# A hybrid two-layer trunk on one core: the order of its instructions from another simulator

## The chip, the cores and the metric

The kernel runs on one core of a Trainium2 chip, as one launch. The metric is the device time of one execution in microseconds (us); lower is better. Engines are named as in the profile: PE is TensorE's matmuls, PEld its weight loads, DVE is VectorE, ACT is ScalarE, POOL is GpSimd, and SP is SyncE, whose queue issues the DMAs.

## The reference

512 tokens of width 1024 pass two layers. Layer 0 mixes tokens with a Mamba-2 SSD block (inner width 2048, 32 heads in 4 groups, state 128, chunks of 128 tokens), layer 1 with HGRN2 (8 heads of 128). Each layer then has a layer norm, a squared-ReLU MLP of width 4096, a second layer norm, and a gate with per-layer input embeddings. All data is float32. Cut to what matters:

```python
for i in range(2):
    mix = ssd_mixer(x, ...) if i == 0 else hgrn2_mixer(x, ...)
    h = layer_norm(ALPHA * x + mix, ln_g[i, 0], ln_b[i, 0])
    h = layer_norm(ALPHA * h + square(relu(h @ w1[i])) @ w2[i], ln_g[i, 1], ln_b[i, 1])
    x = h + sigmoid(h @ ple_w_gate[i]) * (p[i] @ ple_w_proj[i])

# ssd_mixer: z, xbc, dt = split(x @ w_in); xbc = silu(causal_conv(xbc))
#   per chunk and head: y = (C B^T * decay) @ (x dt) + C @ carried_state + d * x
#   out = group_rms_norm(y * silu(z)) @ w_out
# hgrn2_mixer: q, f, v, g = split(x @ w_in); k = (1-lb) sigmoid(-f)
#   per head: causal scores of q and k under products of the forget gates, o = scores @ v
#   out = (rms_norm(o) * silu(g)) @ w_out
```

## The kernel before, in words

**Arithmetic.** Matmuls with weights are made to near float32 accuracy from three fast ones. A value is split into a rounded high part and a low rest, and `mm3` (L118 to L121) adds high x high, high x low and low x high in PSUM: the lines L119, L120 and L121. `unit` (L102) loads a 128 x 1024 weight tile with a DMA on SP's queue (`raw`, 3 buffers, L106) and `split` (L109) makes its high part on ScalarE (`whi`, L113) and its low part on VectorE (`wlo`, L115), with 6 buffers of each. A unit feeds 24 matmuls of 512 columns in `project` and 12 in a block product.

**Stages**, in program order:

- The SSD mixer. Input columns are projected tile by tile (`projected`, which calls `project`), convolved (`conv_silu`, L631 and L634) and passed to `core(j)`, 16 passes of two heads each. A pass transposes (`pt`, L693), weighs (`xw`, L700), makes chunk states (`pm`, L705), carries them (`pv`, L712 to L715), builds decays (L709, L721, L724), and makes two products (`yd` at L735, `yo` at L741) that end in `y` (L748 to L751) and a split (L800, L801). The pass of one pair of heads is traced behind the projections of the next. The block's output product adds into `acc` (L253).
- `norm` and `layer_norm` (L199 to L224), and `transpose_split` (L233, L237, L238), which brings the normalized rows back as split columns.
- The MLP: hidden tiles (L414, L416), then block products with sums of blocks on both sides (seven products in place of eight): `half_blocks` (L293 to L313) prepares the hidden side, `weight_sums` (L315 to L333) loads weights into `r` tiles and adds them on VectorE. `PERIODS` alternates hidden tiles and products. Then the gate (L487 to L499).
- `values4`, the first value products of the HGRN mixer, made in the same way.
- The HGRN mixer: `hcore` handles two heads at a time, four times. It climbs seven levels of growing blocks (L942 to L1046: short matmuls at L972, L980 and L987, VectorE products at L999 to L1012, copies by ScalarE at L1040 and L1046), makes states (L1054 to L1069), outputs (L1078 to L1090) and splits (L1098 to L1100). Between its steps, at 13 `yield`s per pair, `fill` issues background matmuls (projections of later heads, values, the output product) to an amount given in microseconds by `FILL`.
- The second layer norm, MLP and gate, and the output.

**What sets the order.** Nothing above fixes the engines' lists by itself. The kernel is traced as a program with tiles from pools; the tile scheduler then decides. It plays the program in a simulator. Whenever an engine there can take an instruction, it takes the one of best priority among those whose inputs are ready and whose output tile has a free buffer. The priority is the place in the traced program, moved forward by `tc.high_priority(offset=...)`: `LEAD` = 100 places for weight units, `SOON` = 40 for some evictions, `EARLY` = 60, `SUMS` up to 300 for the weight sums, `FIRST` = 1000 for the start. The order in which instructions left, engine by engine, becomes the program; semaphore waits are added after that, and on the chip each engine goes through its list as it stands.

Two parts are under a manual order for TensorE alone, `values4` and the whole HGRN mixer:

```python
with tc.manual_schedule(engines={mybir.EngineType.PE}):
```

There TensorE's list is the traced order; ScalarE, VectorE and SP remain with the scheduler.

## Time and profile before

| | us |
|---|---|
| median of 3 runs | 1425.95 |
| lowest and highest of the runs | 1424.66, 1426.19 |
| the profiled execution, its own time | 1424.0 |
| its span, first to last instruction | 1422.2 |
| PE busy | 1412.7 |
| PEld busy | 1172.5 |
| DVE busy | 1055.1 |
| ACT busy | 754.2 |

How to read it: the span is what the trace covers, and the execution's own time is 1.8 us longer. Busy times of different engines lie beside each other. PE's busy time has modelled ends, since matmuls are pipelined, so it alone doesn't tell whether TensorE works at its full pace. In the rows of the profile, a group is given by line, engine, operation and tiles; "idle before" is the time that the engine stood still just before the group's instructions, followed by what ended it. "Waits" have the total, the number of times and the longest.

### The profile page before, as it was taken

How to read it: one execution, taken by the hardware profiler on the slowest of the kernel's cores; microseconds unless marked ns; L12 is line 12 of the kernel's file. 1: busy time of each engine (PE TensorE's matmuls, PEld its weight loads, DVE VectorE, ACT ScalarE, POOL GpSimd, SP SyncE). 2: the span in 40 equal slices, each digit the busy share in tenths (PEclk: the TensorE clock that was granted, in tenths of full speed). 3: DMA queues.
4: the chain of work that ended last, by engine and by line, in shares of the span. 5: the costliest groups of instructions: out<-in, count | busy, mean ns of one | idle time of the engine just before them, and what ended most of it. 6: DMA issues, size and time to landing. Idle time of an engine off the chain costs nothing.

```text
span 1422.2 us, 20042 instructions
## 1 busy us (share of the span) xinstructions
PE 1412.7 (99%) x7869; PEld 1172.5 (82%) x7869; DVE 1055.1 (74%) x1736; ACT 754.2 (53%) x1134; POOL 1.9 (0%) x12
## 2 busy tenths in 40 slices
PE   9999999999999999999999999999999999999998
PEld 7888888888888888888888888877898888888887
DVE  8998687797966767677986576678695867667873
ACT  7776454563265454545545556655555444544641
POOL 0000000000000000000000000000000000000000
PEclk9999999999999999999999999999999999999999
DMA  8432323233333434344621421222163444434231
GB/s 313 138 124 90 120 87 121 102 115 127 145 119 120 161 133 149 133 146 166 214 83 49 133 90 60 75 90 90 46 236 104 148 140 142 149 133 163 89 119 45
DMA packets 49390, 178.00 MB, mean 125 GB/s; under 512 B 5520, under 2 KB 6288, under 8 KB 49168
## 3 DMA queue, kind: packets, MB, share of 16 engines
q1 hardware_dynamic: 49296, 176.73, 36.3%
q8 instruction: 62, 1.02, 0.3%
q14 instruction: 32, 0.26, 0.1%
HBM read 174.54 MB, written 2.16 MB: 124 GB/s over the span
## 4 chain that ended last, share of the span: by engine, by line
PE 94%; DVE 2%; ACT 2%; DMA 1%; issue 0%; ACTq 0%; DVEq 0%
PE pj L119 24%; PE pj L120 24%; PE pj L121 24%; PE py L119 5%; PE py L121 5%; PE py L120 5%; PE py L735 1%; PE pt L233 1%; PE py L741 1%; PE pm L705 1%; DMA raw<-in_wssd 1%; PE py L972 1%; PE pt L693 1%; PE py L1078 1%; DVE wlo L115 0%
## 5 line engine op out<-in xcount | busy, mean ns | idle before, releaser
L113 ACT CAST whi<-raw 128x1024 fp32r<-128x1024 f32 x222 | 232.9, 1051 | 323.5 <-PE pj L120 225.1
L119 PE MATMUL pj<-b,whi 128*128 128x512 f32 (+1 forms) x1006 | 382.3, 381 | 0.7 <-ACT b L237 0.7
L120 PE MATMUL pj<-b,whi 128*128 128x512 f32 (+1 forms) x1006 | 380.3, 378 | 0.0
L121 PE MATMUL pj<-b,wlo 128*128 128x512 f32 (+1 forms) x1006 | 379.3, 377 | 0.0
L115 DVE TENSOR_TENSOR wlo<-raw,whi 128x1024 fp32r<-128x1024 f32 x222 | 270.0, 1221 | 126.4 <-ACT whi L113 124.6
L119 PEld LDWEIGHTS pj<-b,whi 128*128 128x128 f32 x1006 | 188.8, 188 | 34.2 <-ACT b L237 0.9
L121 PEld LDWEIGHTS pj<-b,wlo 128*128 128x128 f32 x1006 | 189.1, 188 | 33.7
L120 PEld LDWEIGHTS pj<-b,whi 128*128 128x128 f32 x1006 | 189.2, 188 | 32.8 <-issue 0.9
L119 PE MATMUL pj<-whi,b 128*128 128x512 f32 x536 | 213.0, 398 | 0.0
L121 PE MATMUL pj<-whi,b 128*128 128x512 f32 x544 | 212.9, 392 | 0.0
L120 PE MATMUL pj<-wlo,b 128*128 128x512 f32 x536 | 210.2, 392 | 0.0
L121 PEld LDWEIGHTS pj<-whi,b 128*128 128x128 f32 x544 | 102.1, 188 | 21.0
L119 PEld LDWEIGHTS pj<-whi,b 128*128 128x128 f32 x536 | 100.7, 188 | 20.7 <-ACT b L1099 0.6
L120 PEld LDWEIGHTS pj<-wlo,b 128*128 128x128 f32 x536 | 100.8, 188 | 19.3
L113 ACT CAST whi<-r 128x1024 fp32r<-128x1024 f32 x72 | 75.8, 1053 | 67.7 <-PE pj L121 38.6
L115 DVE TENSOR_TENSOR wlo<-r,whi 128x1024 fp32r<-128x1024 f32 x72 | 87.7, 1220 | 20.6 <-ACT whi L113 19.9
L121 PE MATMUL py<-whi,b 128*128 128x512 f32 (+1 forms) x250 | 97.0, 388 | 0.0
L120 PE MATMUL py<-wlo,b 128*128 128x512 f32 x224 | 87.1, 389 | 0.0
L119 PE MATMUL py<-whi,b 128*128 128x512 f32 x224 | 87.1, 390 | 0.0
L121 PEld LDWEIGHTS py<-whi,b 128*128 128x128 f32 x250 | 46.9, 188 | 9.7
L634 DVE SCALAR_TENSOR_TENSOR cv<-pj,cst,cv 128x509 f32<-128x509 f32 (+2 forms) x66 | 48.7, 745 | 3.5 <-ACT cv L631 2.8
L119 PEld LDWEIGHTS py<-whi,b 128*128 128x128 f32 x224 | 42.0, 188 | 9.1 <-DVE sg L494 0.3
(292 smaller groups left out, 1850.8 us busy)
## 6 DMA issues: line engine op xcount, KB each, us to landing
raw<-in_w SPq DMA_DIRECT2D x112, 512.0 KB, 3.7
r<-in_w SPq DMA_DIRECT2D x64, 512.0 KB, 4.1
raw<-in_wssd SPq DMA_DIRECT2D x36, 512.0 KB, 3.8
a<-csd SPq DMA_DIRECT2D x16, 512.0 KB, 3.7
raw<-in_wso SPq DMA_DIRECT2D x16, 512.0 KB, 3.6
raw<-in_wg SPq DMA_DIRECT2D x16, 512.0 KB, 3.7
raw<-in_whq SPq DMA_DIRECT2D x16, 512.0 KB, 3.8
raw<-in_whvg SPq DMA_DIRECT2D x14, 512.0 KB, 3.7
```

Of the source, the lines that this page charges most:

```text
L113: nc.scalar.copy(hi[:, :n], f)
L115: nc.vector.tensor_sub(lo[:, :n], f, f32(hi[:, :n]))
L119: nc.tensor.matmul(out, sh, mh, start=start, stop=False, **kw)
L120: nc.tensor.matmul(out, sh, ml, start=False, stop=False, **kw)
L121: nc.tensor.matmul(out, sl, mh, start=False, stop=stop, **kw)
L233: nc.tensor.transpose(pt[:, j * P : (j + 1) * P], src[:, k * P : (k + 1) * P], ident)
L634: nc.vector.scalar_tensor_tensor(cv[:, d:], ps[:, : T - d], convw[:, i, k : k + 1], cv[:, d:], ALU.mult, ALU.add)
L693: nc.tensor.transpose(pt[:, c * P : (c + 1) * P], xs[:, c * P : (c + 1) * P], ident)
L705: nc.tensor.matmul(pst_[:, c * P : (c + 1) * P], btok[:, c, :], xw[:, c].rearrange("p h q -> p (h q)"), start=True, stop=True)
L735: nc.tensor.matmul(yd[64 * r : 64 * r + 64, sl], xdt[:, 2 * c + r, :], m[:, r, sl], start=True, stop=True)
L741: nc.tensor.matmul(yo[:, c * P : (c + 1) * P], pv[:, c - 1].rearrange("p h q -> p (h q)"), cm[:, c * P : (c + 1) * P], start=True, stop=True,)
L972: nc.tensor.matmul(pcs[r][bs, n * c : n * c + n], kk[r][:, ts], qs, start=True, stop=True)
```

## The change

One argument is given to the context in which the kernel is traced. The scheduler then plays the program in its other simulator, which keeps a timeline of events for each engine, its sequencer, its queues and the DMA engines, with semaphore waits and with times of its own for instructions and transfers. The rule of choice (best priority among what is ready), the program, the tiles, the buffers and the priorities are as before. The parts with a manual order for TensorE keep it.

```diff
@@ -1234,7 +1234,7 @@
     args["csd"] = nc.dram_tensor("csd", (32, T), F32).ap()
     args["out"] = nc.dram_tensor("out_0", (T, D), F32, kind="ExternalOutput").ap()
-    with _tile.TileContext(nc) as tc:
+    with _tile.TileContext(nc, schedule_with_timeline_sim=True) as tc:
         trunk(tc, args)
     r = _run(nc, [feeds], core_ids=[0])
```

## The prediction

> **What bounds the kernel now.** I read the page first: its span, the busy times, the slices of the granted clock and the chain of work that ended last.
>
> ```profile
> span 1422.2 us, 20042 instructions
> PE 1412.7 (99%) x7869; PEld 1172.5 (82%) x7869; DVE 1055.1 (74%) x1736; ACT 754.2 (53%) x1134; POOL 1.9 (0%) x12
> ...
> PEclk9999999999999999999999999999999999999999
> ...
> PE 94%; DVE 2%; ACT 2%; DMA 1%; issue 0%; ACTq 0%; DVEq 0%
> ```
>
> TensorE is the bound: busy for 99% of the span, 94% of the chain, with a granted clock of nine tenths or more in every slice. But its ends are modelled, so I asked the timeline whether "busy" hides slow issue. This is a quiet stretch late in the first mixer:
>
> ```profile
> 366.11 0.39 PE L119 MATMUL pj<-whi,b 128*128 128x512 f32 x1
> ...
> 366.34 0.39 PE L120 MATMUL pj<-wlo,b 128*128 128x512 f32 x1
> ...
> 366.57 0.39 PE L121 MATMUL pj<-whi,b 128*128 128x512 f32 x1
> 366.57 0.19 PEld L119 LDWEIGHTS pj<-whi,b 128*128 128x128 f32 x1
> ...
> 366.79 0.39 PE L119 MATMUL pj<-whi,b 128*128 128x512 f32 x1
> ```
>
> A 512-wide matmul starts every 0.227 us (0.68 us over three), and 0.19 us of each interval is its weight load. No order of the same matmuls changes that.
>
> [...]
>
> Next, the busy times by stretch, which I cut at the seams of the code: start, SSD mixer, first layer norm, MLP and gate with the value products, HGRN mixer, second seam, second MLP and gate, tail.
>
> ```profile
> core 0: us, PE busy (x) PEld busy (x) DVE busy (x) ACT busy (x) POOL busy (x), PEclk, DMA share, GB/s
> 0.00:16.00 16.00, 14.55 (x59) 11.47 (x59) 10.74 (x19) 10.09 (x18) 0.58 (x8) 1.00 0.88 339
> 16.00:370.00 354.00, 353.78 (x1986) 292.72 (x1986) 291.15 (x551) 205.49 (x272) 0.00 (x0) 1.00 0.37 128
> 370.00:390.00 20.00, 18.68 (x149) 17.79 (x148) 19.65 (x27) 6.21 (x11) 0.00 (x0) 1.00 0.33 106
> 390.00:830.00 440.00, 440.00 (x2007) 365.33 (x2007) 315.53 (x386) 231.58 (x304) 1.28 (x4) 1.00 0.40 133
> 830.00:1005.00 175.00, 172.66 (x1728) 140.21 (x1727) 125.83 (x375) 103.25 (x252) 0.00 (x0) 1.00 0.24 80
> 1005.00:1025.00 20.00, 19.71 (x98) 15.56 (x96) 13.48 (x35) 8.37 (x25) 0.00 (x0) 1.00 0.04 16
> 1025.00:1400.00 375.00, 375.00 (x1772) 314.24 (x1771) 274.31 (x341) 187.43 (x251) 0.00 (x0) 1.00 0.40 138
> 1400.00:1422.20 22.20, 18.30 (x87) 15.21 (x85) 4.38 (x8) 1.79 (x3) 0.00 (x0) 0.98 0.14 48
> sum 1422.20, PE 1412.68 PEld 1172.54 DVE 1055.07 ACT 754.23 POOL 1.86; mean PE 176.58 PEld 146.57 DVE 131.88 ACT 94.28 POOL 0.23
> ```
>
> TensorE is idle for 1422.20 - 1412.68 = 9.5 us in all: 1.45 at the start, 3.90 in the tail, and between them 0.22 + 1.32 + 2.34 + 0.29 = 4.17 us. The two MLP stretches, 815 us together, have none. So a new order has about 4 us to win and a whole kernel to lose.
>
> **The change part by part.** The program keeps its instructions, tiles and priorities. What moves is the order in which each engine's list is written, since that is the order in which the simulator let the instructions go. On the chip each engine runs its list as written; a wait at its head holds all that is queued behind it. So an edit costs something only where an instruction stands ahead of one that the chip could have run sooner, and only if TensorE then has nothing ready.
>
> *The weight feed, all stretches.* Each weight unit is a DMA on SP's queue (L106), a cast on ScalarE (L113) and a difference on VectorE (L115).
>
> ```profile
> L113 ACT CAST whi<-raw 128x1024 fp32r<-128x1024 f32 x222 | 232.9, 1051 | 323.5 <-PE pj L120 225.1
> L115 DVE TENSOR_TENSOR wlo<-raw,whi 128x1024 fp32r<-128x1024 f32 x222 | 270.0, 1221 | 126.4 <-ACT whi L113 124.6
> raw<-in_w SPq DMA_DIRECT2D x112, 512.0 KB, 3.7
> ```
>
> Refilling one unit takes 3.7 + 1.05 + 1.22 = 6.0 us from issue. How far ahead it runs is seen in what the casts waited for:
>
> ```profile
> L113 ACT CAST whi<-raw x222: 1029/1055/1068, 16.8 to 1389.7; 128x1024 fp32r<-128x1024 f32 x111
> L113 ACT CAST whi<-r x72: 1037/1055/1057, 436.0 to 1333.0; 128x1024 fp32r<-128x1024 f32 x72
> its engine sat idle before it (us, times) until:
>   PE pj L120: 232.4, 85
>   PE pj L121: 99.7, 59
>   PE py L121: 45.6, 49
> ```
>
> In 85 + 59 + 49 = 193 of 294 casts ScalarE stood waiting for TensorE to give a buffer back: the feed is held back by its six buffers. A unit feeds 24 matmuls (5.4 us at 0.227) in a projection and 12 (2.7 us) in a product, so five filled buffers are 14 to 27 us of work, against 6.0 us to refill. A cast or a load that is moved a few places, or an SP wait that holds the next loads a few us, stays hidden. I put the feed, and with it both MLP stretches, at 0. If that cover went, each missing unit would show up to 6.0 us.
>
> *SSD mixer (16 passes, TensorE's order also free).* TensorE visits each pass's short matmuls between projections that depend on nothing in the pass. A visit written too early waits for VectorE or ScalarE with the projections stuck behind it. Now such waits are small:
>
> ```profile
> PEld pm L705 <- DVE xw L700: 1.9, 11, 0.2
> PEld pt L693 <- ACT btok L662: 1.5, 4, 0.6
> ```
>
> Lower end: those 3.4 us and no more vanish. Upper end: each pass waits for one L115 that was put ahead of its operation, 16 x 1.22 = 19.5 us. I take one wait of L693's size per pass, 16 x (1.5 / 4) = 6.0 us, because visits placed with a margin are what the rows show; that is nearer to a small slip than to a whole L115.
>
> *HGRN mixer (4 pairs of heads, TensorE's order stays as traced).* Here only ScalarE, VectorE and SP move, while TensorE's list, with its fixed portions of background matmuls between the steps, does not. A pair has 13 such hand-overs, 52 in all. Lower end: the 2.34 us idle of that stretch are won. Upper end: an L115 ahead of the chain at every hand-over, 52 x 1.22 = 63 us. I take one per pair, 4 x 1.22 = 4.9 us; VectorE has 175.0 - 125.8 = 49 us unused there, so most displaced differences find a gap.
>
> *Table loads on ScalarE.* They sit between functions, and a new order can bring more or fewer.
>
> ```profile
> L709 ACT ACT_TABLE_LOAD x14 | 18.0, 1283 | 0.2
> ...
> 1004.07 0.22 ACT L1085 ACTIVATION_READ_ACCUMULATOR cbm<-py 128x1 f32 x1
> ...
> 1004.30 1.28 ACT L1086 ACT_TABLE_LOAD   x1
> ...
> 1005.60 0.30 ACT L1086 ACTIVATE hms<-hms,cst 128x4 f32<-128x4 f32 x1
> ```
>
> One costs 1.28 us on an engine that is 53% busy. It matters only as a late step of a chain, where it weighs like one L115, so it is inside the bounds above; I add 0.
>
> [...]
>
> *Seams, start and tail.* At the first layer norm VectorE is busy 19.65 of 20 us, and TensorE idles 1.32. The step there that could be displaced is this pair:
>
> ```profile
> L223 DVE SCALAR_TENSOR_TENSOR acc<-acc,lnmv,a 128x1024 f32<-128x1024 f32 x16 | 20.4, 1277 | 0.3 <-DVE lnmv L218 0.3
> L224 DVE SCALAR_TENSOR_TENSOR acc<-acc,lnrs,b 128x1024 f32<-128x1024 f32 x16 | 20.4, 1278 | 0.0
> ```
>
> Bounds -1.3 to +2.6 us; I take 0, and 0 for the start and the tail, where data in and out set the time.
>
> Sum: 6.0 + 4.9 = 10.9 us. The profiled execution took 1424.0 us (1422.2 of span and 1.8 around it), so 1434.9; the median of the runs, 1425.95, lies 1.95 above that execution, so I forecast 1436.9.
>
> **Rivals.** *Faster.* The other simulator's order suits the chip's timing better and TensorE's inner waits close. For it: greedy filling with projections is always possible in the SSD mixer. Against: only 4.17 us are there, 2.34 of them under a frozen TensorE list. It gives 1425.95 - 4.2 = 1421.8, by at most these 4 us.
>
> *No change.* Either the two orders nearly agree, or the buffers swallow every difference. For it: 193 blocked casts and no idle TensorE over 815 us. Against: two mixers whose short steps have no such buffers. It gives 1426.
>
> *The HGRN list breaks (slower, and outside my range).* The chain of a pair alternates between TensorE, VectorE and ScalarE, and the portions of background between steps are fixed. If the new order puts weight splits or evictions of the background ahead of chain steps as a rule, not once per pair, every hand-over waits. At 32 of 52 hand-overs it is 39 us, at all of them 63: 1425.95 + 6.0 + 63 = 1495. For it: the chain steps have the better priority only when they are ready in the simulator's own time. Against: VectorE's 49 spare us. It decides from about 8 displaced hand-overs on (8 x 1.22 = 10 us).
>
> [...]
>
> **How the numbers follow.** A modest loss as summed: 50%. The HGRN list breaks: 18%. No change: 15%. Faster: 17%. A measurement of this kernel tells about 0.2% (2.9 us) from no change; the runs spread from 1424.66 to 1426.19. The modest loss by itself runs from 1429 to 1475: above, SSD's 19.5, half the HGRN bound (27 of 63 would be 22 hand-overs) and a seam's 2.6 on 1425.95. Below, I let the range reach to 1420, the faster rival with the runs' spread. That leaves out most of the broken-list case above (about 13%) and a few per cent below.
>
> **What would show it.** In the changed kernel's profile: about 7869 matmuls again, the same 0.227 us pace, no idle TensorE in both MLP stretches (feed term 0). In the SSD stretch, waits of TensorE's weight loads on L700, L662 or L721 grown by about 6 us; in the HGRN stretch TensorE idle of about 7 instead of 2.34 us, ended by VectorE or ScalarE. I am wrong if the loss lies in the MLP stretches (the cover was not there), if a seam or the start is longer by over 3 us, if TensorE's clock falls, or if TensorE idles less than 7 us in all.

## The result, and the profile after

| us | before | after |
|---|---|---|
| median (lowest to highest of 4 runs each) | 1426.07 (1424.66 to 1427.10) | 1504.36 (1502.71 to 1507.23) |
| the profiled execution, its own time | 1424.0 | 1507.23 |
| its span | 1422.2 | 1505.5 |

The ratio is 1.0552, 95% interval 1.0531 to 1.0572. The forecast was 1436.9, its range 1420 to 1475: the sign was right, the size was not, and the time lies outside the range. The page of the changed kernel, the lines that answer to those shown first of before:

```profile
span 1505.5 us, 20089 instructions
PE 1440.5 (96%) x7869; PEld 1191.2 (79%) x7869; DVE 1055.7 (70%) x1736; ACT 777.6 (52%) x1151; POOL 1.9 (0%) x12
...
PEclk9999999999899999999989999999989999999999
...
PE 84%; DVE 9%; ACT 4%; issue 2%; DMA 1%; DVEq 0%; ACTq 0%
```

The same 7869 matmuls and 1736 VectorE instructions, but TensorE's share of the chain fell from 94% to 84%, VectorE's rose from 2% to 9%, and three of the 40 slices of the granted clock dropped to 8. TensorE is idle for 1505.5 - 1440.5 = 65.0 us (before 9.5), and its busy time grew by 1440.5 - 1412.7 = 27.8. The two, 55.5 + 27.8 = 83.3, are the whole growth of the span.

The busy times by stretch of the changed kernel say where. I cut it at its own seams, which come later and later than those of before (columns as in the table of before; the seventh entry of each row, after the five engines, is the granted clock):

```profile
16.00:60.00 44.00, 37.31 (x219) 30.25 (x219) 31.54 (x60) 34.84 (x42) 0.00 (x0) 0.92 0.53 196
60.00:370.00 310.00, 304.67 (x1652) 250.23 (x1651) 238.36 (x459) 186.40 (x236) 0.00 (x0) 0.99 0.30 101
370.00:393.50 23.50, 23.50 (x117) 19.22 (x116) 17.68 (x26) 8.12 (x11) 0.00 (x0) 1.00 0.62 224
393.50:420.00 26.50, 8.64 (x37) 6.75 (x37) 24.68 (x32) 4.16 (x8) 0.00 (x0) 0.61 0.25 79
420.00:433.00 13.00, 12.32 (x103) 11.89 (x102) 2.08 (x3) 1.89 (x4) 0.00 (x0) 1.00 0.01 1
433.00:750.00 317.00, 317.00 (x1442) 264.27 (x1441) 227.65 (x273) 158.46 (x201) 0.00 (x0) 1.00 0.44 143
750.00:770.00 20.00, 12.70 (x49) 9.54 (x49) 16.41 (x26) 8.20 (x17) 0.00 (x0) 0.74 0.54 157
770.00:820.00 50.00, 50.00 (x239) 41.30 (x238) 25.59 (x33) 21.11 (x30) 0.00 (x0) 1.00 0.17 54
820.00:840.00 20.00, 14.90 (x63) 11.62 (x62) 14.56 (x17) 11.69 (x18) 0.00 (x0) 0.83 0.16 56
840.00:1070.00 230.00, 227.69 (x1966) 186.02 (x1965) 153.76 (x411) 133.51 (x284) 1.28 (x4) 1.00 0.27 86
1070.00:1125.00 55.00, 42.48 (x231) 36.44 (x230) 38.74 (x69) 20.36 (x52) 0.00 (x0) 0.84 0.34 125
1125.00:1440.00 315.00, 315.00 (x1436) 262.87 (x1435) 221.91 (x269) 158.75 (x203) 0.00 (x0) 1.00 0.41 132
```

Length less PE busy is the idle time. The long matmul streams (433 to 750, 770 to 820, 1125 to 1440) have none, as before. Five short places have most of it: the start of the SSD 6.7, the first norm 17.9 + 0.7, the second norm 7.3, the transposes of the value products (L448) 5.1, the end of the HGRN mixer with the third norm 12.5. Each of them also has a granted clock below 1.0. The SSD between 60 and 370 has 5.3, and the body of the HGRN mixer 2.31, where before had 2.34.

TensorE's waits in the changed kernel (total, times, longest) name the same places:

```profile
PE pt L233 <- DVE b L238: 19.6, 6, 5.3
PE pt L233 <- issue: 8.7, 1, 8.7
PE pj L119 <- ACT b L237: 6.4, 5, 3.7
PE pj L119 <- ACT sz L683: 5.3, 3, 2.2
PE pt L448 <- DVE b L453: 4.9, 2, 3.0
PE py L666 <- ACT cm L635: 4.5, 1, 4.5
PE pt L233 <- DVE acc L224: 2.4, 1, 2.4
```

L233 is the transpose of the normalized rows in `transpose_split`, L237 and L238 its two evictions, L224 the last step of `layer_norm`: a few waits of several us, at seams, and not many small ones.

What happens there is read best from VectorE's timeline at the first norm (start, duration, instruction). First before, then after:

```profile
357.34 0.15 DVE L221 RECIPROCAL lnrs<-lnsd 128x1 f32<-128x1 f32 x1
357.41 0.73 DVE L253 SCALAR_TENSOR_TENSOR acc<-pj,ri,acc 128x512 f32<-128x512 f32 x1
358.06 1.28 DVE L224 SCALAR_TENSOR_TENSOR acc<-acc,lnrs,b 128x1024 f32<-128x1024 f32 x1
```

```profile
393.61 0.21 DVE L221 RECIPROCAL lnrs<-lnsd 128x1 f32<-128x1 f32 x2
393.74 1.20 DVE L327 TENSOR_TENSOR r<-r,r 128x1024 f32<-128x1024 f32 x1
394.87 0.68 DVE L207 BATCH_NORM_STATS2 lnst<-acc 128x6 f32<-128x512 f32 x1
395.47 1.20 DVE L115 TENSOR_TENSOR wlo<-raw,whi 128x1024 fp32r<-128x1024 f32 x1
396.59 0.74 DVE L253 SCALAR_TENSOR_TENSOR acc<-pj,ri,acc 128x512 f32<-128x512 f32 x1
397.26 1.21 DVE L330 TENSOR_TENSOR r<-r,r 128x1024 f32<-128x1024 f32 x1
398.39 2.35 DVE L115 TENSOR_TENSOR wlo<-raw,whi 128x1024 fp32r<-128x1024 f32 x2
400.66 0.74 DVE L253 SCALAR_TENSOR_TENSOR acc<-pj,ri,acc 128x512 f32<-128x512 f32 x1
401.32 2.46 DVE L224 SCALAR_TENSOR_TENSOR acc<-acc,lnrs,b 128x1024 f32<-128x1024 f32 x2
```

VectorE is never idle in either (busy 2.00 of 2.00 us from 357.34 to 359.34 before, 10.17 of 10.17 from 393.61 to 403.78 after). But between the reciprocal L221 and the L224 that needs it, before has one other instruction listed and after has eight (nine between the first L221 and its own L224): sums of weights (L327, L330), weight splits (L115), other rows' statistics (L207), output parts (L253). L224 starts 401.32 - 393.74 = 7.6 us later than it could. In TensorE's timeline over the same time the output product is used up and nothing else is left until the rows arrive (in brackets the idle time and what ended it):

```profile
393.56 0.39 PE L121 MATMUL pj<-whi,b 128*128 128x512 f32 x1
402.69 1.09 PE L233 MATMUL pt<-cst,acc 128*128 128x128 f32 x4 [8.74 <-issue]
409.11 1.12 PE L233 MATMUL pt<-cst,acc 128*128 128x128 f32 x4 [5.33 <-DVE b L238]
413.30 1.12 PE L233 MATMUL pt<-cst,acc 128*128 128x128 f32 x4 [3.08 <-DVE b L238]
```

In before the first of these transposes ran at 359.44 among output parts that were still left. "issue" in the first row stands for a wait with no releaser in the profile. By the times it was L224: the first of the two from 401.32 (1.23 us each) ends 0.1 us before 402.69.

Eight or nine instructions stand there only in the first two rows of the first norm. At the second and third norm L221 and L224 are about as close as before (0 to 4 instructions between them, before 1 to 3). At the second, the transposes start when TensorE's products have run out (the first L233 at 756.42, after 2.36 us of waiting; in before at 701.16, among products); what makes them late there was not taken apart.

### The profile page after: what moved, and what is told of

The parts are those of the page before. It is cut to its first block, busy times and chain, and to the rows that moved or that the text cites. A ratio compares the mean times of both kernels' runs of the same rounds, so it can differ in the third digit from the quotient of the medians.

```text
span 1505.5 us, 20089 instructions
## 1 busy us (share of the span) xinstructions
PE 1440.5 (96%) x7869; PEld 1191.2 (79%) x7869; DVE 1055.7 (70%) x1736; ACT 777.6 (52%) x1151; POOL 1.9 (0%) x12
## 4 chain that ended last, share of the span: by engine, by line
PE 84%; DVE 9%; ACT 4%; issue 2%; DMA 1%; DVEq 0%; ACTq 0%
PE pj L119 22%; PE pj L120 21%; PE pj L121 21%; PE py L119 4%; PE py L120 4%; PE py L121 4%; DVE wlo L115 2%; PE py L735 1%; PE pt L233 1%; DVE acc L223 1%; PE py L741 1%; DMA acc<-in_x 1%; DVE acc L224 1%; PE pm L705 1%; PE py L972 0%
## 5 line engine op out<-in xcount | busy, mean ns | idle before, releaser
L115 DVE TENSOR_TENSOR wlo<-raw,whi 128x1024 fp32r<-128x1024 f32 x222 | 270.4, 1219 | 143.1 <-ACT whi L113 141.9
L119 PE MATMUL pj<-whi,b 128*128 128x512 f32 x536 | 216.3, 405 | 9.9 <-ACT sz L683 5.3
L121 PE MATMUL pj<-whi,b 128*128 128x512 f32 x544 | 215.9, 400 | 0.0
L119 PEld LDWEIGHTS pj<-whi,b 128*128 128x128 f32 x536 | 102.7, 192 | 31.8 <-ACT sz L683 5.8
L121 PEld LDWEIGHTS pj<-whi,b 128*128 128x128 f32 x544 | 104.1, 192 | 21.5
L115 DVE TENSOR_TENSOR wlo<-r,whi 128x1024 fp32r<-128x1024 f32 x72 | 87.5, 1218 | 18.5 <-ACT whi L113 18.3
L121 PEld LDWEIGHTS py<-whi,b 128*128 128x128 f32 x250 | 46.9, 188 | 9.7
L237 ACT CAST b<-pt 128x512 fp32r<-128x512 f32 x32 | 18.7, 584 | 68.6 <-PE pt L233 68.6
L634 DVE SCALAR_TENSOR_TENSOR cv<-pj,cst,cv 128x509 f32<-128x509 f32 (+2 forms) x66 | 49.2, 745 | 6.4 <-ACT cv L631 5.3
```

What stands on the lines that cost most here:

```text
L115: nc.vector.tensor_sub(lo[:, :n], f, f32(hi[:, :n]))
L119: nc.tensor.matmul(out, sh, mh, start=start, stop=False, **kw)
L121: nc.tensor.matmul(out, sl, mh, start=False, stop=stop, **kw)
L237: nc.scalar.copy(h, v)
L634: nc.vector.scalar_tensor_tensor(cv[:, d:], ps[:, : T - d], convw[:, i, k : k + 1], cv[:, d:], ALU.mult, ALU.add)
```

## The experiments

Theories were about where the loss is made. P: TensorE's list. V: the lists of VectorE and ScalarE. W: the engines of the other simulator take in instructions ahead of their turn, so that a step that becomes ready later is listed behind all that was taken in. T: the other simulator's times of single instructions. L: each stretch's own lists make the loss seen there, against C (carried from stretch to stretch) and M (transfers and buffers).

**Whose list.** "Tied" means an ordering edge, without any synchronisation, from each listed instruction of an engine to the next, so that the scheduler must emit the given list:

```diff
     with _tile.TileContext(nc, schedule_with_timeline_sim=True) as tc:
         trunk(tc, args)
+        _pin(nc, tc)
+def _pin(nc, tc):
+    traced = {i.name: i for i in nc.cur_bb.bb.instructions}
+    info = mybir.DependencyInfo(mybir.DependencyClass.NoSync, mybir.DependencyReason.DATA)
+    for e in _ORDERS:                       # the engines whose list is given
+        order = [traced[n] for n in _listed(e) if n in traced]
+        for x, y in zip(order, order[1:]):
+            tc.add_manual_dep(y, x.name, info, reason="listed order")
```

*All three engines.* The changed kernel with PE, DVE and ACT tied to the lists of before:

> The changed kernel, with TensorE, VectorE and ScalarE all tied to the order of before; only SP's list and the choice of buffers come from the other simulator. Both theories: 1424 to 1432 us. If instead SP's list carries the loss (a third theory, loads that come late), well over 1440 us with waits on transfers.

Measured 1424.30, ratio 0.9992 (0.9981 to 1.0003). With the old lists the change costs nothing: SP's list and the choice of buffers, which stay with the other simulator, carry none of the loss.

*TensorE alone.* `_ORDERS` of before with PE only, in the changed kernel:

> The changed kernel, with TensorE's matmuls tied to the order they had before the change; ScalarE, VectorE and SP stay with the other simulator. Theory P (the loss sits in TensorE's own list: short matmuls and transposes written too late, so that the projections that should cover them are spent): about 1425 to 1445 us, transposes at the seams spread out again, TensorE idle under 20 us. Theory V (the loss sits in VectorE's and ScalarE's lists: weight work put ahead of the norm's steps): 1475 to 1510 us, TensorE still idle some 20 us at the first norm.

Measured 1490.64, ratio 1.0449 (1.0418 to 1.0479): 14 of 78 us come back, which is in V's range and not in P's. The reverse, the kernel before with TensorE tied to the changed kernel's list:

> The reverse: the kernel before, with TensorE's matmuls tied to the order that the other simulator gave them; ScalarE, VectorE and SP are placed by the first simulator around that list. Theory P: 1480 to 1510 us. Theory V: 1426 to 1445 us.

Measured 1477.70, ratio 1.0358 (1.0328 to 1.0388). TensorE's new list alone costs 51 us, though taking it away gives back only 14; this run is in neither range. P falls as it was put: the parts do not add.

*VectorE and ScalarE.* The changed kernel with DVE and ACT tied to the lists of before:

> The changed kernel, with VectorE and ScalarE tied to the order they had before; TensorE and SP stay with the other simulator. Theory P: 1480 us or more, the seams lose as much as in the changed kernel. Theory V: 1425 to 1445 us.

Measured 1550.10, ratio 1.0865 (1.0834 to 1.0897): slower still. TensorE's waits of that run:

```profile
PE pj L119 <- ACT sz L683: 36.7, 5, 8.9
PE pj L119 <- DVE cv L634: 14.0, 3, 9.0
```

TensorE's list, which the other simulator still makes, asks for L683 and L634 sooner than the old lists of the other two engines bring them. V falls as it was put: undoing an engine does not measure its share. The other direction, the kernel before with DVE alone tied to the changed kernel's list:

> The kernel before, with VectorE's instructions tied to the order that the other simulator gave them; the first simulator places TensorE, ScalarE and SP around it. If VectorE's late norm steps lose time by themselves: 1450 to 1490 us, most of it at the norms. If they only hurt together with TensorE's late transposes: under 1440 us.

Measured 1506.01, ratio 1.0565 (1.0534 to 1.0595), above both ranges. TensorE's longest waits, at the norms, are those of the changed kernel:

```profile
PE pt L233 <- DVE b L238: 19.1, 5, 5.3
PE pt L233 <- issue: 8.5, 1, 8.5
```

VectorE's list is enough to make a loss of the whole size, also when the old simulator orders everything else. Elsewhere the waits are partly others: the one at L666 is gone, and L987 waits 3.2 us.

**Why the lists differ.** The other simulator lets each engine hold instructions that have been taken in and not begun. How many is a setting of the scheduler, and no trace shows such a number for the chip. One edit sets other depths ("all 2" here):

```diff
+    from concourse.hw_specs import TRN2Spec as _spec
+    _spec.ENG_ISSUE_QUEUE_DEPTH = {e: 2 for e in _spec.ENG_ISSUE_QUEUE_DEPTH}
     nc = _bacc.Bacc("TRN2", ...
```

All engines at 1:

> The changed kernel, but the other simulator lets an engine hold only 1 instruction (TensorE 35 and the others 12 in the changed kernel). Theory W (an engine of the other simulator takes in instructions well before it runs them, so whatever becomes ready later, short matmuls and norm steps, is written behind them): most of the 78 us come back, 1425 to 1450 us, and the seams lose under 15 us together. Theory T (its times of single instructions and transfers are what misplaces things): 1480 us or more.

Measured 1654.72, ratio 1.1608 (1.1546 to 1.1670), a miss. VectorE's list did what W says, with nothing left between L221 and L224. But the SSD got much worse, and at the norms L233 still waits, 24.3 us for L224, 19.0 for L238 and 17.2 as "issue". The cause was not shown: TensorE and SP were both held to 1 here, and the two were not tried apart. The longest wait:

```profile
PE pm L705 <- DVE xw L700: 39.1, 15, 4.2
```

These are the states of the SSD passes, which wait 15 times. All engines at 2:

> As before with 2 instructions held per engine. Theory W: within 15 us of the run with 1. Theory T: 1480 us or more.

Measured 1466.02, ratio 1.0284 (1.0254 to 1.0314): 38 of 78 us come back. It is far from the run with 1, against what was expected of W, and below T's range. TensorE at 2, the others at 12 as they were:

> TensorE holds 2, the others keep 12. Theory W with TensorE's 35 as the larger share (35 matmuls are 8 us of work at 0.227 us): 1430 to 1465 us. If the others' 12 is the larger share: 1465 to 1500 us. Theory T: 1480 us or more, like both others.

Measured 1477.63, ratio 1.0366 (1.0333 to 1.0399). TensorE at 35 as it was, the others at 2:

> TensorE keeps 35, the others hold 2. Theory W with TensorE's share the larger: 1465 to 1500 us, and the last mixer passes and first transposes stay as late in TensorE's list as in the changed kernel. If the others' share is the larger: 1430 to 1465 us.

Measured 1480.61, ratio 1.0387 (1.0356 to 1.0417). Each half gives back about a third (27 and 24 us), both together 38. TensorE at 2, VectorE and ScalarE at 1:

> The changed kernel; TensorE may hold 2 instructions, VectorE and ScalarE 1 (SP keeps 12). With 2 held on VectorE one more operation still got in behind nearly every step of the norms. Theory W alone: 1430 to 1448 us, and the seams lose under 12 us together. If what is left of the loss at 2 held (some 40 us) has another cause, the other simulator's times: 1452 to 1475 us.

Measured 1448.74, ratio 1.0163 (1.0133 to 1.0192): 1504.4 - 1448.7 = 55.6 us come back, 0.7 us short of W's range. SP keeps 12 here and had 2 in "all 2", so the gain over that run need not come from VectorE and ScalarE alone. TensorE at 8, VectorE and ScalarE at 1:

> The same with TensorE holding 8. Theory W: each matmul held ahead costs where TensorE has little other work; between the run with 2 and the one with 35, so 8 to 15 us above the run with 2, with the transposes of the first norm a few us later in TensorE's list. If TensorE's window matters only past some dozen: within 4 us of the run with 2.

Measured 1459.47, ratio 1.0238 (1.0208 to 1.0268): deeper TensorE costs 10.7 us more. W holds for about 56 of the 78 us. The depths show in VectorE's list: between L221 and its L224 stand 9, 9, 3, 1, 4 and 3 instructions in the changed kernel's first six rows, 2 or 4 with all engines at 2, none with all at 1; in before 1 or 2. It is not VectorE's own depth alone: with VectorE still at 12 and TensorE at 2 the first two rows have 2 and 6, and in the best of these runs, VectorE at 1 and TensorE at 2, the six rows have 2, 2, 5, 5, 5 and 3. How far TensorE runs ahead in the simulator shapes VectorE's list too, and this one count does not rank the runs.

*Times of single instructions.* window_2_1_1, with the other simulator's own read times taken out (they are then as in the first one) and its write-back tails behind an operation set to 0; both are times of that simulator, and no trace shows them:

```diff
+    _spec.TIMELINE_SIM_ACCESS_CYCLES = {}
+    _spec.TIMELINE_SIM_WRITE_TAIL_CYCLES = {k: 0 for k in _spec.TIMELINE_SIM_WRITE_TAIL_CYCLES}
+    _spec.TIMELINE_SIM_ACTIVATE_EXTRA_TAIL_CYCLES = 0
+    _spec.PE_WRITE_TAIL_NS = 0.0
```

> As window_2_1_1, and the other simulator's own times of reads and of the write-back behind an operation on VectorE, ScalarE and TensorE are taken out (reads as the first simulator has them, no tails). Theory T for the rest of the loss: results that land late in the simulator let other work in first, so 10 to 25 us below window_2_1_1. Theory W: within 6 us of it.

Measured 1449.60, ratio 1.0169 (1.0139 to 1.0198), within 1 us of the run without this edit. T falls for these times; other times of that simulator were not tried.

**Local or carried.** There are points inside the first MLP stretch and late in the SSD up to which each engine's two lists hold the same instructions. There the lists can be spliced, all three engines together:

```diff
+    # _ORDERS[e] = before's list up to 550 us of before + the changed kernel's list from there
```

> The changed kernel, with the lists of TensorE, VectorE and ScalarE tied to those of the kernel before from the start to the instruction that runs at 550 us in the kernel before (inside the first MLP stretch, where the same instructions lie ahead of the cut in both kernels); behind it the changed kernel's own lists. Theory L (the loss is made where the trace shows it, each stretch by its own lists): the changed kernel's trace has 20.5 us of loss over the kernel before up to 275 us of the old time, 24.1 from there to 550, 38.5 behind it, so this kernel gives back 44.6 and takes 1460 us (1455 to 1466). Rival C (an engine that runs ahead or late in one stretch sets the loss of the next, so the parts cannot be told apart): the sum does not close; the remaining loss differs from 38.5 by more than 8 us.

Measured 1462.13, ratio 1.0253 (1.0220 to 1.0285): 42.2 come back, 44.6 expected. Then before's lists only from 275 to 550 us:

> The changed kernel, with the three engines tied to the lists of the kernel before only between 275 and 550 us of the old time (the last group of the SSD and the first norm); ahead of it and behind it the changed kernel's own lists. Theory L: 24.1 us come back, 1480 us (1475 to 1486), and TensorE's waits for the transposes of the first norm are gone from the trace. Rival C: the first norm is late because the lists ahead of it had made VectorE late; then it stays late with the old lists and less than 12 us come back, over 1492.

Measured 1479.20, ratio 1.0372 (1.0342 to 1.0402): 25.2 come back, 24.1 expected, and the waits of L233 at this norm, 8.7 and 8.4 us in the changed kernel, are down to one short one. The stretches of that run across the norm:

```profile
366.00:393.00 27.00, 27.00 (x140) 22.59 (x141) 24.52 (x37) 6.83 (x12) 0.00 (x0) 1.00 0.44 167
393.00:406.00 13.00, 11.65 (x97) 11.21 (x97) 13.00 (x17) 3.65 (x6) 0.00 (x0) 1.00 0.43 139
406.00:420.00 14.00, 14.00 (x105) 13.35 (x104) 9.83 (x10) 9.80 (x14) 0.00 (x0) 1.00 0.37 119
```

1.35 us idle, as before (1.32), at full clock, although the SSD up to 275 us still has the new lists. L holds and C falls: the norm, with the end of the SSD ahead of it, makes its own loss. The same cut for what is left in window_2_1_1, first before's lists up to 550 us:

> What is left in window_2_1_1 (1448.7 us, 22.7 over the kernel before): its trace has 9.2 us of loss over the kernel before up to 275 us, 6.6 from there to 550, 7.6 behind it. Here the three engines are tied to the lists of the kernel before up to 550 us, and to the lists of window_2_1_1 behind it. Theory L: 15.8 us come back, 1433 us (1430 to 1437). Rival M (the rest is not in the lists of these three engines but in when the transfers are issued and which buffers are used): nothing comes back, 1445 to 1452.

Measured 1433.59, ratio 1.0058 (1.0027 to 1.0089): 15.1 come back. Then the other half:

> The other half of the run before it: the lists of window_2_1_1 up to 550 us, those of the kernel before behind it. Theory L: 7.6 us come back, 1441 us (1438 to 1445). Rival M: 1445 to 1452. If the two halves give back 22.7 us together, the rest of the loss is in the lists and spread over the whole program, and no single place makes it.

Measured 1440.15, ratio 1.0098 (1.0069 to 1.0128): 8.6 come back, 15.1 + 8.6 = 23.7 of 22.7. M falls: the rest is in the lists too and spread over the program. What in the other simulator makes these last 23 us was not found. No list tried beats that of before.

## Why the prediction was wrong

**The weight feed, 0: right.** All three long streams kept TensorE full, at the pace of before (317.00 us for 1442 matmuls from 433 on, 0.220 us each; before 440.00 for 2007, 0.219), with casts, splits and loads reordered. TensorE's own list is the same in both kernels over most of the two MLP streams (439 to 710 us and 1133 to 1403 us).

**"Seams, start and tail ... I take 0": the step that failed.** The bounds, -1.3 to +2.6 us at the first norm, came from counting what could be displaced (one pair L223, L224) and not what could be put ahead of it. The lists put eight or nine instructions ahead, 7.6 us on VectorE, at the first rows of a norm whose later rows the quoted table showed at 19.65 of 20 us. TensorE idles 17.9 us there instead of 1.32, and the stretch from the end of the SSD over the norm gave back 25 us when its lists were put back. The third norm, with the end of the HGRN mixer, idles 12.5. The start of the program, up to 16 us, stayed at 1.45, as the term had it.

**"Both MLP stretches at 0": half wrong.** The stretch that I called MLP and gate also holds the second norm and the turn of its rows into value products. Both have the same chain (L224, L233, L238; L448, L453), and they idle 7.3 + 5.1 = 12.4 us. Because they were quiet in before, the table by stretch hid that they are seams.

**SSD, 6.0 us: mis-sized.** Up to 275 us of the old time, the start included, the matmul starts of the changed kernel fall 20.5 us behind those of before, just above the upper end of 19.5 without the start. The size came from waits of weight loads, 3.4 us in all, while TensorE itself idled only 0.22 us in that stretch. The assumed shape, one small wait in each of 16 passes, was wrong too: about 10 us are lost at the start (6.7 of them idle, 4.5 in one wait of L666 for ScalarE's L635), and about 4 at each of two borders between groups of passes (148 and 244 us), where TensorE waits 2.2 us for ScalarE's L683 and then runs at half clock (0.50 from 149.9 to 153.3, 0.52 from 245.4 to 248.8). The interior of the passes loses little, by these figures some 2.5 us.

**"Table loads on ScalarE ... I add 0": not nothing in the changed kernel.** It has 69 of them, before 52, and the 17 more are all in the SSD mixer. One stands right ahead of the L683 that TensorE waits for at 148 us, and the same at 244:

```profile
146.63 1.28 ACT L683 ACT_TABLE_LOAD   x1
147.92 0.60 ACT L683 ACTIVATE sz<-pj 128x512 f32<-128x512 f32 x1
```

So 1.28 of the 2.2 us of that wait is a load. What the 17 cost together was not tried. Their number does not set the loss: the run with TensorE at 35 and the others at 2 also has 69, and up to 275 us of the old time it loses only 3.6 us.

**HGRN, 4.9 us, and the rival that its list breaks: wrong place.** Its body idles 2.31 us against 2.34 before. With TensorE's order unchanged there and background between the steps, VectorE's 49 spare us were enough, as the argument against the rival said. The end of the mixer does wait, 2.0 us for L1090 at L1098. TensorE's order, which the prediction took as fixed for the whole mixer, is the old one only up to 1060 us (997 of before): the background matmuls that stand in front of L1098 in before have been moved ahead.

**The price of an idle microsecond.** The sum took idle time at its face value. The growth of the span is 83.3 / 55.5 = 1.5 times that of the idle time, and the clock is the larger part of the difference. A falling clock was named as a sign of being wrong and given no price. These rows of the changed kernel show the fall:

```profile
399.10:419.60 20.50, 7.79 (x31) 0.50 0.25 83
419.60:421.00 1.40, 1.40 (x13) 1.00 0.00 0
```

The first norm's stall began at 393.95; the clock was granted 0.50 from 399.1 (5.2 us later) to 419.6, and was full again 4.5 us after work without a pause began at 415.1. Over the span the clock is at half for 68.3 us, and TensorE is busy in 40.4 of them. A 512-wide matmul starts every 0.43 us there (149.9 to 153.3) and not every 0.227, so by an estimate from these figures 40.4 x (1 - 0.227 / 0.43) = 19 of the 27.8 us of longer busy time are the clock's. Where the other 9 come from was not found.

**Rivals.** Faster and no change are ruled out by the interval. The rival on the slow side had the right unit, instructions listed ahead of a late chain step, and put it in the mixer with spare VectorE time and fixed background in place of the norms with neither. That its highest price, 1495, lies near the 1504 measured is luck.

## What to carry to other kernels

When a change reorders lists, look for the places where the bounding engine has only one chain left to wait for (norms, transposes at a stage's end), even if they are quiet now, and price there a whole run of listed instructions of the busy neighbour, not one. The long streams here, with filled buffers and TensorE's list as it was, shrugged off the reordering of the other engines (no idle time in 317, 50 and 315 us). Lists of several engines belong together: putting one or two engines' old lists back gave 14 and -46 us, and TensorE's new list alone cost 51, shares that cannot all hold, while splicing all of them at a common point gave parts that add up.

## What the hardware showed that I had not expected

The clock also fell after a stall of 2.23 us. At 148.57 us in the changed kernel TensorE resumes after waiting that long for L683, at full clock; 1.3 us later the clock is halved for 3.4 us:

```profile
148.57 0.50 PE L119 MATMUL pj<-whi,b 128*128 128x512 f32 x1 [2.23 <-ACT sz L683]
```

```profile
149.00:149.90 0.90, 0.90 (x6) 1.00 0.00 0
149.90:153.30 3.40, 3.40 (x11) 0.50 0.00 0
153.30:155.00 1.70, 1.70 (x11) 0.99 0.00 0
```

The same is seen again after a stall of 2.23 us that ends at 244.37 (0.52 from 245.4 to 248.8). Here the penalty comes after the stall, when the trace shows TensorE fully busy again (3.40 of 3.40 us at 0.50), so it appears as busy time and in no list of waits. In the 5 us ahead of the stall TensorE ran mostly matmuls of 64 and 128 columns; whether they had a part in the fall was not tried.

The starts of the half-clock stretches of this trace tell more. They are 44.12, 149.93, 245.50, 399.10, 757.50, 829.18, 1074.94 and 1102.25 us, all whole multiples of 3.413 us apart, and each lasts 1, 2, 3 or 6 times 3.413 us. So the span of this run can be cut into cells of 3.413 us, and what the clock did in one went with how idle the cell before it was. Some of these cells (length, busy time of TensorE, clock):

```profile
146.52:149.93 3.41, 1.36 (x6) 1.00 0.37 143
392.28:395.69 3.41, 1.66 (x8) 1.00 0.00 0
395.69:399.10 3.41, 0.00 (x0) 1.00 0.41 115
1071.53:1074.94 3.41, 1.44 (x13) 1.00 0.32 126
1095.42:1098.84 3.42, 1.58 (x10) 1.00 0.46 155
```

After the first, third and fourth the clock is halved, after the second and fifth not. In the changed kernel every full-clock cell inside the program with 1.97 us idle or more is followed by half clock and none with 1.75 or less; in between, one with 1.77 is and one with 1.83 is not. At half clock, cells with 0.78 us idle or more kept it there, and cells with at most 0.11 ended it. So in this trace somewhat over half a cell of idle time was enough (1.77 to 2.23 us of 3.413) if it fell into one cell.
